# Streaming encoder layer: the convolution's last inputs stored as columns by six DMAs, and memory keys' turns, last sums and first second-layer weight splits put in another order

## The chip, the cores and the metric

The kernel runs on one core of one Trainium2 chip. The metric is the device time of one execution in microseconds (us). The time before is 979.41 us, the median of three runs (978.93 to 979.56). Engines are named as in the profile: PE is TensorE's matmuls and PEld its weight loads, DVE is VectorE, ACT ScalarE, POOL GpSimd, SP SyncE, which here only issues DMAs. A "q" behind an engine's name (SPq, ACTq) marks an instruction of its sequencer, such as a DMA's issue.

## The reference

One layer of an encoder serves two groups at once: a prompt of 512 rows and a sample of 64 rows with caches, both of width 1024, with shared weights, all in float32. What matters here:

- `proj = rmsnorm(x) @ w_in` gives, among others, 1536 channels for a short causal convolution over 4 rows. Beside its result the convolution returns its last three input rows, `conv_new = xp[:, L:]`, a (3, 1536) array for each group. These are two of the outputs.
- The convolved channels feed a gated-delta attention with 4 heads (in chunks of 64 rows). A second attention takes the difference of two softmaxes, normalizes each head's result by its root mean square, and both together go through `w_out` and are added to `x`.
- A cross attention to 256 memory rows follows. For the prompt, its keys and values are projected from the memory: `(m @ wk, m @ wv)`, two (256, 1024) arrays that are also outputs.
- Then `h + relu(hn @ w_ff1)^2 @ w_ff2` with 4096 hidden channels, and a last rmsnorm.

## The kernel before

**Layout.** Activations are kept with channels on the 128 partitions and the 576 rows (512 + 64) along the free dimension. To keep float32's accuracy with the faster float32r matmuls, an operand is split in a high part (a cast on ScalarE) and a low part (the rest, a subtraction on VectorE), and three products are added: high x high, high x low, low x high. `split_weights` (line 155 on) loads a block of weights through SyncE, casts it (line 161) and subtracts (line 162); `project` runs the matmuls of a block of 128 output channels over the rows in two halves (256 and 320) and hands the two results in PSUM to a function that evacuates them. Nearly all matmuls have line 107, the helper `mm`; nearly all turns (transposes on TensorE with an identity) line 113, the helper `tr`.

**PSUM.** The eight banks carry tags: three "pr" for projections, two "ba" for turns and small products, and one each of "g0", "g1" and "gs".

**The order of the work** isn't written out by hand for most of the kernel. The framework takes each instruction's place in the text as its priority and makes one fixed order per engine from it, with its own estimate of when inputs are ready; `tc.high_priority()` lifts a block, `pin` keeps a matmul behind the earlier ones of its engine, and `tc.issue_after(ins)` queues those instructions of a block that run on `ins`'s engine behind `ins`, in order of issue only. At run time each engine, and each DMA queue, takes its instructions in that fixed order and waits at each for its inputs and buffers.

**The convolution's last inputs.** For each of the 12 blocks of 128 channels, GpSimd copies the last three prompt columns and the last three sample columns into `cst`, a [128, 12, 6] tile (lines 461 and 462). After the gate values `gg` and `beta` (up to line 551), the loop at line 553 turns four blocks at a time into a "ba" bank, six rows by 512, copies them to SBUF on VectorE (line 558), and stores three rows to each group's output through SyncE (lines 559 and 560). Around it in time stand the turns of the gate columns (`abT`, line 502 and after, read by TensorE through line 113), the gate chain on VectorE and ScalarE (lines 507 to 551), and the projection of `z` (`project_z`).

**The last attention head and the memory.** `diff_head` works off one head of the second attention, leaves each tile's sum of squares in `so` and its result in `on`, and returns `finish`, which makes the scaling factors (line 1103, then the power on GpSimd, line 208), scales `on` (line 1105), turns it with five turns in two "ba" banks and writes `od` (line 1111). The loop over `w_mem_k` and `w_mem_v` (from line 1137) projects the memory in two column halves `f`. Each half takes four blocks of weights (`kc`), twelve matmuls each. The result is copied to `tokens` (line 1153); a half of the keys is then turned, four turns per "ba" bank and two banks per half, and each bank is split into high and low part (`split_turned`, lines 1131 and 1132); then the half is stored (line 1166). `finish` of the last head comes after the second half of the keys. While the values' first half is done, `od` is split (lines 201 and 202).

**The feed-forward block.** The first layer is done in 16 pairs of output blocks (`ff1_pair`), each with seven products in banks "ba", "gs" and "g1" (a fast scheme with seven products in place of eight). Intermediate results are kept by copies on ScalarE (`keep`, line 1462), and four `put`s do the additions, relu, square and the split of the result (lines 1470 to 1477). The second layer's weights come by `weights2`: a load into one of three `r` buffers (line 1432), a cast (line 1426) and a subtraction (line 1427). From the fourth block on they are split with high priority.

**The end.** The last rmsnorm needs the sums of squares of each row. `final_roots` adds, for the last three row tiles, the sum over `accs[0]` and the sum over the last block's squares (`more`) in one PSUM group, with one matmul each per row tile, then scales (line 1579), takes the power on GpSimd (line 208), and `put_out` scales the turned rows (lines 1563 and 1565) and stores them.

Of the kernel before, what the change touches and what calls it, by code (L numbers as in the profile page):

```python
# [11 lines left out]
ALU = mybir.AluOpType  # L12
# [25 lines left out]
def hybrid_layer_kernel(  # L38
# [61 lines left out]
    def bank(tag="ba"):  # L100
        return ps.tile([P, 512], F32, tag=tag, name=nm(tag), bufs=BANKS[tag])
# [448 lines left out]
    V.reciprocal(beta, t1)  # L550
    halves_of(beta2, beta)

    for j in range(3):
        b = bank()
        for i in range(4):
            tr(b[:6, i * P : (i + 1) * P], cst[:, 4 * j + i, :])
        cso = small("ko", [6, 512])
        V.tensor_copy(cso, b[:6, :])
        nc.sync.dma_start(o_conv_p[0, 0][:, j * 512 : (j + 1) * 512], cso[0:3])
        nc.sync.dma_start(o_conv_s[0, 0][:, j * 512 : (j + 1) * 512], cso[3:6])  # L560

    gsum = bank()
    ggf = gg.rearrange("p c h -> p (c h)")
# [496 lines left out]
    def diff_head(h, between):  # L1060
# [5 lines left out]
        for t in (4, 0, 1, 2, 3):  # L1066
# [32 lines left out]
            A.activation(pr[1][:, :P], po, AF.Square, accum_out=so[:, t : t + 1])  # L1099
            A.copy(on[:, t, :], po)  # L1100

        def finish():
            V.tensor_scalar(so, so, 1.0 / P, EPS, ALU.mult, ALU.add)
            rpow(co, so)
            V.tensor_tensor(on, on, co.unsqueeze(2).to_broadcast([P, 5, P]), ALU.mult)
            b, b2 = bank(), bank()
            for t in range(4):
                tr(b[:, t * P : (t + 1) * P], on[:, t, :])
            tr(b2[:, :P], on[:, 4, :])
            for src, ts_ in ((b, slice(0, SEQ)), (b2[:, DEC:P], slice(SEQ, T))):  # L1110
                A.activation(od[:, h, ts_], src, AF.Identity, scale=dn)
# [22 lines left out]
    mkv = pair(1, F32R)  # L1134
    mkT, mv, tokens = view(mkv, 0, KT, NMEM), view(mkv, 1, 2, D), view(e3, 1, 2, D)
    mkl, mvl = lows("At0", "At1", "Dt0", "Dt1"), lows("Y0", "Y1", "B1", "B1")
    for w, out in ((w_mem_k, o_mk), (w_mem_v, o_mv)):
        dst = tokens
        for f in range(2):
            fs = slice(512 * f, 512 * f + 512)  # L1140
            bs = [bank("pr") for _ in range(2)]
            for kc in range(4):
                wt = split_weights(w[0, 256 * kc : 256 * kc + 256, fs], [P, 2, 512])
                for k in (2 * kc, 2 * kc + 1):
                    for t in range(2):
                        ts_ = slice(t * P, (t + 1) * P)
                        for j, (wi, x) in enumerate(((0, mh), (0, ml), (1, mh))):
                            mm(
                                bs[t], x[:, k, ts_], wt[wi][:, k % 2, :],
                                start=(k == 0 and j == 0), stop=(k == KT - 1 and j == 2),  # L1150
                            )
            for t in range(2):
                (A.copy if t else V.tensor_copy)(dst[:, t, fs], bs[t])
                if out is o_mv:
                    A.copy(mv[:, t, fs], dst[:, t, fs])
                    V.tensor_tensor(mvl[2 * t + f], dst[:, t, fs], mv[:, t, fs].bitcast(F32), ALU.subtract)
            if out is o_mk:
                for i in range(2):
                    b = bank()
                    for j in range(2):  # L1160
                        m = 4 * f + 2 * i + j
                        for t in range(2):
                            tr(b[:, j * 256 + t * P : j * 256 + (t + 1) * P], dst[:, t, m * P : (m + 1) * P])
                    m = 4 * f + 2 * i
                    split_turned(mkT[:, m : m + 2, :], mkl[m // 2].rearrange("p (j n) -> p j n", j=2), b)
            nc.sync.dma_start(out[0, 0].rearrange("(b p) h d -> p b (h d)", p=P)[:, :, fs], dst[:, :, fs])
            if out is o_mk and f == 1:
                finish()
            if out is o_mv and f == 0:
                ob = pair(5, F32R)  # L1170
                for h in range(H):
                    split_to((ob,), od[:, h, :], h, 0)
# [249 lines left out]
    def split(src, tag, bufs, urgent):  # L1422
        shape = list(src.shape)
        wh, wl = (ft(tag + x, shape, bufs, F32R) for x in "hl")
        with tc.high_priority() if urgent else ExitStack():
            A.copy(wh, src)  # L1426
            V.tensor_tensor(wl, src, wh.bitcast(F32), ALU.subtract)  # L1427
        return wh, wl
# [4 lines left out]
        return split(raw, "w2", 3, urgent)  # L1433

    NG, SCALED = 8, 5

    def ff1_pair(p, sx):
        ws = parts.pop(p)
# [53 lines left out]
        put(1, N1, s3, s5)  # L1492
        product(4, x, False)
        put(1, N0, x[:, :NH], None)
        if p + 1 < 2 * NG:
            split_pair(p + 1)
        if p + 2 < 2 * NG:
# [72 lines left out]
    def final_roots(ts, pin=False, more=None):  # L1570
# [2 lines left out]
        r, r2 = tiny([P, 8]), tiny([P, 8])  # L1573
        for i, t in enumerate(ts):
            q0, n = QT[t]
            mm(b[:, t : t + 1], accs[0][:, q0 : q0 + n], ones[:, 0:1], stop=more is None, pin=pin and i == 0)
            if more is not None:
                mm(b[:, t : t + 1], more[:, q0 - 256 : q0 - 256 + n], ones[:, 0:1], start=False)
        V.tensor_scalar(r[:, c], b[:, c], 1.0 / D, EPS, ALU.mult, ALU.add)  # L1579
        rpow(r2[:, c], r[:, c])  # L1580
        return r2

# [97 lines left out]
```

## Time and profile before

| | |
|---|---|
| runs | 978.93, 979.41, 979.56 us |
| profiled execution | 979.89 us |
| its span, from the first to the last instruction | 978.2 us |
| mean granted clock of TensorE | 0.997 |
| last matmul's end | about 8 us before the end of the span |

The profiled execution is one that the hardware profiler recorded; its own time stands 1.7 us above its span. A row of a timeline gives the start in us from the span's start, the duration in us, the engine, the line of the kernel, the operation, output and inputs by tile name, the shapes, the number of instructions merged in the row, and in brackets the idle time of the engine just before, with the instruction whose end ended it. A wait is put down to what came last. Matmuls run pipelined, so their rows overlap; the distance between starts says what one costs.

### The profile page before, as it was taken

How to read it: one execution, taken by the hardware profiler on the slowest of the kernel's cores; microseconds unless marked ns; L12 is line 12 of the kernel's file. 1: busy time of each engine (PE TensorE's matmuls, PEld its weight loads, DVE VectorE, ACT ScalarE, POOL GpSimd, SP SyncE). 2: the span in 40 equal slices, each digit the busy share in tenths (PEclk: the TensorE clock that was granted, in tenths of full speed). 3: DMA queues.
4: the chain of work that ended last, by engine and by line, in shares of the span. 5: the costliest groups of instructions: out<-in, count | busy, mean ns of one | idle time of the engine just before them, and what ended most of it. 6: DMA issues, size and time to landing. Idle time of an engine off the chain costs nothing.

```text
span 978.2 us, 16971 instructions
## 1 busy us (share of the span) xinstructions
PE 960.9 (98%) x6399; PEld 889.0 (91%) x6399; DVE 691.4 (71%) x1540; ACT 537.4 (55%) x1218; POOL 57.5 (6%) x125
## 2 busy tenths in 40 slices
PE   9999999999999999999999999999999999999996
PEld 7999999898888878999999998999999999999996
DVE  6655777867767676666657797567867779978674
ACT  7665785444557675445445567665544445545444
POOL 3441020101000000000000000000000000000000
PEclk9999999999999999999999999999999999999998
DMA  7432432121654656341121423322222223233202
GB/s 216 124 124 76 114 105 66 33 55 40 179 132 132 231 159 197 86 130 44 52 58 44 141 70 93 87 87 86 87 87 86 86 87 87 86 88 86 65 23 97
DMA packets 124915, 96.01 MB, mean 98 GB/s; under 512 B 6204, under 2 KB 112846, under 8 KB 124322
## 3 DMA queue, kind: packets, MB, share of 16 engines
q1 hardware_dynamic: 124466, 94.28, 33.2%
q8 instruction: 50, 0.82, 0.3%
q10 hardware_dynamic: 368, 0.66, 0.2%
q14 instruction: 31, 0.25, 0.1%
HBM read 79.93 MB, written 9.75 MB: 92 GB/s over the span
## 4 chain that ended last, share of the span: by engine, by line
PE 86%; DVE 5%; ACT 3%; issue 2%; DMA 2%; POOL 1%; POOLq 0%; ACTq 0%; DVEq 0%; SPq 0%
PE pr L107 53%; PE g L107 11%; PE ba L107 10%; PE gs L107 6%; PE ba L113 3%; PE g L113 2%; DMA raw<-in_w_ff_dram 1%; DMA r<-in_w_ff_dram 1%; POOL tg L208 1%; DVE wl L162 1%; DMA raw<-in_w_mem_o_dram 1%; ACT wh L161 0%; DVE w L1326 0%; PE gs L113 0%; DVE on L808 0%
## 5 line engine op out<-in xcount | busy, mean ns | idle before, releaser
L107 PE MATMUL pr<-u,wh 128*128 128x320 f32 (+2 forms) x1240 | 326.5, 341 | 1.4 <-DVE zr L195 0.9
L107 PEld LDWEIGHTS pr<-u,wh 128*128 128x128 f32 x1240 | 211.9, 188 | 16.9 <-DVE zr L195 1.1
L107 PE MATMUL pr<-u,wl 128*128 128x256 f32 (+1 forms) x816 | 225.8, 301 | 0.0
L107 PEld LDWEIGHTS pr<-u,wl 128*128 128x128 f32 x816 | 150.0, 189 | 2.2 <-DVE wl L388 0.2
L162 DVE TENSOR_TENSOR wl<-raw,wh 128x1024 fp32r<-128x1024 f32 x65 | 79.5, 1223 | 56.0 <-ACT wh L161 55.8
L161 ACT CAST wh<-raw 128x1024 fp32r<-128x1024 f32 x65 | 68.2, 1050 | 59.9 <-PE pr L107 43.9
L107 PE MATMUL pr<-u,w2h 128*128 128x320 f32 (+1 forms) x384 | 98.5, 340 | 0.0
L1426 ACT CAST w2h<-r 128x512 fp32r<-128x512 f32 x56 | 34.7, 620 | 89.0 <-PE pr L107 85.8
L107 PE MATMUL pr<-f,w2h 128*128 128x320 f32 (+1 forms) x288 | 74.4, 341 | 0.2 <-DVE u L1513 0.2
L107 PEld LDWEIGHTS pr<-u,w2h 128*128 128x128 f32 x384 | 65.0, 188 | 4.5 <-ACT u L1509 0.3
L107 PE MATMUL pr<-u,w2l 128*128 128x256 f32 (+1 forms) x256 | 65.1, 295 | 0.0
L1511 DVE TENSOR_TENSOR u<-u,pr 128x256 f32<-128x256 f32 x96 | 42.4, 450 | 17.0 <-PE pr L107 16.3
L107 PE MATMUL ba<-u,wl 128*128 128x288 f32 x360 | 53.0, 296 | 0.9 <-ACT keep L1462 0.9
L107 PEld LDWEIGHTS pr<-f,w2h 128*128 128x128 f32 x288 | 48.7, 188 | 4.2 <-issue 1.4
L107 PEld LDWEIGHTS ba<-u,wl 128*128 128x128 f32 x360 | 49.2, 188 | 1.7 <-ACT keep L1462 1.6
L107 PE MATMUL pr<-f,w2l 128*128 128x256 f32 (+1 forms) x192 | 48.8, 295 | 0.0
L107 PEld LDWEIGHTS pr<-u,w2l 128*128 128x128 f32 x256 | 46.9, 188 | 1.5
L208 POOL TENSOR_TENSOR tiny<-tiny,nhalf 128x1 f32<-128x1 f32 (+4 forms) x10 | 9.1, 913 | 643.4 <-DVE tiny L1579 531.5
L1427 DVE TENSOR_TENSOR w2l<-r,w2h 128x512 fp32r<-128x512 f32 x56 | 38.5, 688 | 11.2 <-ACT w2h L1426 10.9
L107 PE MATMUL pr<-wh,u 128*128 128x512 f32 x128 | 41.4, 398 | 0.0
L1471 ACT ACTIVATE c<-c 128x288 f32<-128x288 f32 x48 | 20.6, 443 | 29.5 <-DVE c L1470 29.5
L107 PEld LDWEIGHTS pr<-f,w2l 128*128 128x128 f32 x192 | 35.2, 188 | 1.1
(551 smaller groups left out, 2022.2 us busy)
## 6 DMA issues: line engine op xcount, KB each, us to landing
raw<-in_w_ff_dram SPq DMA_DIRECT2D x36, 512.0 KB
raw<-in_w_in_dram SPq DMA_DIRECT2D x28, 512.0 KB
r<-in_w_ff_dram SPq DMA_DIRECT2D x56, 256.0 KB
raw<-in_w_mem_k_dram SPq DMA_DIRECT2D x8, 512.0 KB
raw<-in_w_mem_v_dram SPq DMA_DIRECT2D x8, 512.0 KB
raw<-in_w_out_dram SPq DMA_DIRECT2D x8, 512.0 KB
raw<-in_w_mem_q_dram SPq DMA_DIRECT2D x8, 512.0 KB
raw<-in_w_mem_o_dram SPq DMA_DIRECT2D x8, 512.0 KB
```

The costliest lines, as they stand in the source:

```text
L107: i = nc.tensor.matmul(out, lhsT, rhs, start=start, stop=stop, skip_group_check=skip_group_check)
L113: i = nc.tensor.transpose(out, in_, ident[:n, :n])
L161: A.copy(wh, raw)
L162: V.tensor_tensor(wl, raw, wh.bitcast(F32), ALU.subtract)
L208: G.tensor_tensor(out, in_, bc(nhalf[: in_.shape[0], 0:1], list(in_.shape)), ALU.pow)
L1426: A.copy(wh, src)
L1427: V.tensor_tensor(wl, src, wh.bitcast(F32), ALU.subtract)
L1471: A.activation(c, c, AF.Relu)
L1511: V.tensor_tensor(am, am, b, ALU.add)
```

## The change

Five things are changed.

- The turns of `cst`, their copies and their six stores are gone. Six DMAs on ScalarE's queue write the columns of `cst` directly: for each of the three rows and each group, 128 partitions x 12 numbers, where partition `p` and block `m` go to place `128 m + p` of the output row.
- For the last head, the factors (line 1103 and the power) are traced at the end of `diff_head` instead of in `finish`.
- The turns of the memory keys of a column half are traced in the next half's projection, between its first and second block of weights; the second half's stand in the values' projection, and `finish` of the last head comes behind them. The store of a half no longer stands behind its turns.
- The second-layer splits without high priority (the first three blocks) are queued behind the last instruction of `ff1_pair(1)`'s last `put`, an instruction of VectorE.
- `final_roots` sums `accs[0]` and `more` in two PSUM banks. The first is scaled as before; the second is multiplied and added to it by one VectorE instruction.

```diff
--- before.py
+++ after.py
@@ -550,14 +550,9 @@
     V.reciprocal(beta, t1)
     halves_of(beta2, beta)
 
-    for j in range(3):
-        b = bank()
-        for i in range(4):
-            tr(b[:6, i * P : (i + 1) * P], cst[:, 4 * j + i, :])
-        cso = small("ko", [6, 512])
-        V.tensor_copy(cso, b[:6, :])
-        nc.sync.dma_start(o_conv_p[0, 0][:, j * 512 : (j + 1) * 512], cso[0:3])
-        nc.sync.dma_start(o_conv_s[0, 0][:, j * 512 : (j + 1) * 512], cso[3:6])
+    for i in range(3):
+        for j, dst in enumerate((o_conv_p, o_conv_s)):
+            nc.scalar.dma_start(dst[0, 0, i].rearrange("(m p) -> p m", p=P), cst[:, :, 3 * j + i])
 
     gsum = bank()
     ggf = gg.rearrange("p c h -> p (c h)")
@@ -1099,9 +1094,16 @@
             A.activation(pr[1][:, :P], po, AF.Square, accum_out=so[:, t : t + 1])
             A.copy(on[:, t, :], po)
 
+        def factors():
+            G.tensor_scalar(so, so, 1.0 / P, EPS, ALU.mult, ALU.add)
+            rpow(co, so)
+
+        if h == H - 1:
+            factors()
+
         def finish():
-            V.tensor_scalar(so, so, 1.0 / P, EPS, ALU.mult, ALU.add)
-            rpow(co, so)
+            if h < H - 1:
+                factors()
             V.tensor_tensor(on, on, co.unsqueeze(2).to_broadcast([P, 5, P]), ALU.mult)
             b, b2 = bank(), bank()
             for t in range(4):
@@ -1134,6 +1136,21 @@
     mkv = pair(1, F32R)
     mkT, mv, tokens = view(mkv, 0, KT, NMEM), view(mkv, 1, 2, D), view(e3, 1, 2, D)
     mkl, mvl = lows("At0", "At1", "Dt0", "Dt1"), lows("Y0", "Y1", "B1", "B1")
+    turn_keys = lambda: None
+
+    def key_turns(f, dst):
+        def turn_keys():
+            for i in range(2):
+                b = bank()
+                for j in range(2):
+                    m = 4 * f + 2 * i + j
+                    for t in range(2):
+                        tr(b[:, j * 256 + t * P : j * 256 + (t + 1) * P], dst[:, t, m * P : (m + 1) * P])
+                m = 4 * f + 2 * i
+                split_turned(mkT[:, m : m + 2, :], mkl[m // 2].rearrange("p (j n) -> p j n", j=2), b)
+
+        return turn_keys
+
     for w, out in ((w_mem_k, o_mk), (w_mem_v, o_mv)):
         dst = tokens
         for f in range(2):
@@ -1141,6 +1158,10 @@
             bs = [bank("pr") for _ in range(2)]
             for kc in range(4):
                 wt = split_weights(w[0, 256 * kc : 256 * kc + 256, fs], [P, 2, 512])
+                if kc == 1:
+                    turn_keys()
+                    if out is o_mv and f == 0:
+                        finish()
                 for k in (2 * kc, 2 * kc + 1):
                     for t in range(2):
                         ts_ = slice(t * P, (t + 1) * P)
@@ -1154,18 +1175,8 @@
                 if out is o_mv:
                     A.copy(mv[:, t, fs], dst[:, t, fs])
                     V.tensor_tensor(mvl[2 * t + f], dst[:, t, fs], mv[:, t, fs].bitcast(F32), ALU.subtract)
-            if out is o_mk:
-                for i in range(2):
-                    b = bank()
-                    for j in range(2):
-                        m = 4 * f + 2 * i + j
-                        for t in range(2):
-                            tr(b[:, j * 256 + t * P : j * 256 + (t + 1) * P], dst[:, t, m * P : (m + 1) * P])
-                    m = 4 * f + 2 * i
-                    split_turned(mkT[:, m : m + 2, :], mkl[m // 2].rearrange("p (j n) -> p j n", j=2), b)
             nc.sync.dma_start(out[0, 0].rearrange("(b p) h d -> p b (h d)", p=P)[:, :, fs], dst[:, :, fs])
-            if out is o_mk and f == 1:
-                finish()
+            turn_keys = key_turns(f, dst) if out is o_mk else lambda: None
             if out is o_mv and f == 0:
                 ob = pair(5, F32R)
                 for h in range(H):
@@ -1422,7 +1433,7 @@
     def split(src, tag, bufs, urgent):
         shape = list(src.shape)
         wh, wl = (ft(tag + x, shape, bufs, F32R) for x in "hl")
-        with tc.high_priority() if urgent else ExitStack():
+        with tc.high_priority() if urgent else tc.issue_after(put_last[1]):
             A.copy(wh, src)
             V.tensor_tensor(wl, src, wh.bitcast(F32), ALU.subtract)
         return wh, wl
@@ -1433,6 +1444,7 @@
         return split(raw, "w2", 3, urgent)
 
     NG, SCALED = 8, 5
+    put_last = {}
 
     def ff1_pair(p, sx):
         ws = parts.pop(p)
@@ -1492,6 +1504,7 @@
         put(1, N1, s3, s5)
         product(4, x, False)
         put(1, N0, x[:, :NH], None)
+        put_last[p] = nc.cur_bb.bb.instructions[-1]
         if p + 1 < 2 * NG:
             split_pair(p + 1)
         if p + 2 < 2 * NG:
@@ -1573,10 +1586,14 @@
         r, r2 = tiny([P, 8]), tiny([P, 8])
         for i, t in enumerate(ts):
             q0, n = QT[t]
-            mm(b[:, t : t + 1], accs[0][:, q0 : q0 + n], ones[:, 0:1], stop=more is None, pin=pin and i == 0)
-            if more is not None:
-                mm(b[:, t : t + 1], more[:, q0 - 256 : q0 - 256 + n], ones[:, 0:1], start=False)
+            mm(b[:, t : t + 1], accs[0][:, q0 : q0 + n], ones[:, 0:1], pin=pin and i == 0)
         V.tensor_scalar(r[:, c], b[:, c], 1.0 / D, EPS, ALU.mult, ALU.add)
+        if more is not None:
+            b = bank()
+            for t in ts:
+                q0, n = QT[t]
+                mm(b[:, t : t + 1], more[:, q0 - 256 : q0 - 256 + n], ones[:, 0:1])
+            V.scalar_tensor_tensor(r[:, c], b[:, c], 1.0 / D, r[:, c], ALU.mult, ALU.add)
         rpow(r2[:, c], r[:, c])
         return r2
```

## The prediction

> **What bounds the kernel now.** I read the page's busy shares first, then the waits of TensorE, then the stretches that the change touches. On the page:
>
> ```profile
> span 978.2 us, 16971 instructions
> ...
> PE 960.9 (98%) x6399; PEld 889.0 (91%) x6399; DVE 691.4 (71%) x1540; ACT 537.4 (55%) x1218; POOL 57.5 (6%) x125
> ```
>
> TensorE is busy for 98% of the span; all its idle time, the tail included, is 978.2 - 960.9 = 17.3 us. So a microsecond is won in three ways only: TensorE gets less to do, one of its few waits goes, or the tail after its last matmul gets shorter. Work taken off VectorE (71%) or SyncE is worth nothing by itself. The waits of TensorE that the change can reach:
>
> ```profile
> PE ba L107 <- ACT keep L1462: 1.2, 2, 0.9
> PE ba L113 <- DVE At L1132: 1.1, 1, 1.1
> ```
>
> (Columns: total us, times, longest.) The second is at the turning of the memory keys, the first in the first layer of the feed-forward block. The profiled execution took 979.89 us, 1.7 more than its span; the three timed runs have the median 979.41, 0.5 below it. The terms below are differences inside the span, and I take them off the median.
>
> **The convolution's turns go.** The twelve turns of `cst` in TensorE's timeline, each with the row that follows:
>
> ```profile
> 100.09 0.60 PE L113 MATMUL ba<-ident,cst 128*6 128x128 f32 x4
> 100.53 0.38 PE L113 MATMUL g<-ident,u 128*128 128x128 f32 x2
> ...
> 103.88 1.03 PE L113 MATMUL ba<-ident,cst 128*6 128x128 f32 x8
> 104.67 0.47 PE L107 MATMUL pr<-u,wh 128*128 128x512 f32 x1
> ```
>
> Matmuls overlap, so the price is the distance from start to start: 100.53 - 100.09 = 0.44 for four, 104.67 - 103.88 = 0.79 for eight. TensorE loses **1.23 us** of work. VectorE's three copies of line 558 and SyncE's six issues go too; I count them at nothing, because TensorE doesn't wait for them.
>
> **Six DMAs come to ScalarE's queue.** They can't start before the last `cst` copy (GpSimd's row). What then stands on ScalarE, VectorE and TensorE, and two rows on what an issue costs:
>
> ```profile
> 98.08 0.18 POOL L462 COPY cst<-p 128x3 f32<-128x3 f32 x1
> 99.97 1.05 ACT L161 CAST wh<-raw 128x1024 fp32r<-128x1024 f32 x1 [1.64 <-PE pr L107]
> 101.11 1.20 DVE L162 TENSOR_TENSOR wl<-raw,wh 128x1024 fp32r<-128x1024 f32 x1
> 102.24 0.17 DVE L502 COPY p<-p 16x64 f32<-16x64 f32 x1
> 103.04 0.28 SPq L559 DMA_DIRECT2D out_dram<-p  x1
> 103.14 0.23 PE L113 MATMUL ba<-ident,p 16*128 16x16 f32 x1
> ...
> 971.83 0.92 ACTq L1568 DMA_DIRECT2D out_dram<-u  x2
> ```
>
> The inputs are there at 98.26, and ScalarE is idle for the 1.64 us before 99.97, so I put all six issues there. Queued behind them is the cast at 99.97, behind that on VectorE the low part of the same weights (101.11), behind that in VectorE's order the copy at 102.24, and TensorE's turn at 103.14 needs that copy. With the first four turns of `cst` gone, TensorE comes to it at 103.14 - 0.44 = 102.70; the copy ended at 102.41. So a hold of ScalarE is free for 1.64 + 0.29 = 1.93 us; of each further microsecond TensorE waits all.
>
> What is the hold? ScalarE's own issues took 0.92 for two, with a wait for data between them, so 0.46 each is the upper price; SyncE's store of the same rows took 0.28, the lower. Six hold ScalarE for 1.7 to 2.8 us, and TensorE waits 0 to 0.9. I take **0.5**, the middle. It supposes that the queue takes all six without filling. Whether it does, no row of ScalarE shows. For SyncE's queue the trace shows an issue behind large loads, then the packets from 25.14 to 25.80 us, nearly all of 32 bytes, and those from 98.3 to 107.2, nearly all of 512:
>
> ```profile
> 4.01 0.47 SPq L152 DMA_DIRECT2D raw<-in_w_in_dram  x1
> 4.53 2.49 SPq L129 DMA_DIRECT2D u<-in_x_sample_dram  x1
> ...
> DMA packets 1083, 0.09 MB, mean 134 GB/s; under 512 B 970, under 2 KB 1083, under 8 KB 1083
> ...
> q1 hardware_dynamic: 1083, 0.09, 116.1%
> q1 hardware_dynamic: 2104, 1.07, 45.4%
> ```
>
> An issue of the usual 0.47 us took 2.49 with several loads ahead of it: a full queue holds its issuer. A wide packet costs 45.4% x 16 engines x 8.9 us / 2104 = 30.7 ns. In the other stretch 1.161 x 16 x 0.66 = 12.3 us were spent; less 113 wide ones, the 970 small ones took 9.1 ns each. One new DMA moves 128 x 12 = 1536 single numbers of 4 bytes, 96 on each of 16 engines: 0.87 us at the small price, 2.95 at the wide one. If each issue has to wait for the DMA ahead of it, the hold is 0.46 + 5 x 0.87 = 4.8 us or 0.46 + 5 x 2.95 = 15.2, and TensorE's wait 2.9 or 13.3. So the ends are 0 and 13.3; a hold can't gain anything. I stay at 0.5, by the row of ScalarE's own issues, and carry the rest into the rivals. The weight loads share the engines, but these were taken for 45% of this stretch: six times 0.87 us at the small price fits in.
>
> The Trainium skill, "DMA: Bandwidth & Descriptors", section "Rules for kernel authors", speaks against this edit: a last dimension that isn't contiguous becomes one descriptor per element, and should be rearranged instead; its section "Specifications" adds that a transfer under 512 B is read, modified and written. No row of this trace shows such a narrow write to DRAM, so the trace neither bears this out nor denies it. By about 10.5 ns per packet, from its section "Bandwidth", a new DMA would be an estimated 1.0 us by that page; the rows' 9.1 ns are close to it.
>
> **The memory keys' turns move** behind the first quarter of the next projection, and the last head's `finish` with them. Now:
>
> ```profile
> 361.76 0.65 PE L113 MATMUL ba<-ident,u 128*128 128x128 f32 x4 [1.08 <-DVE At L1132]
> ...
> 359.61 0.83 DVE L1105 TENSOR_TENSOR an<-an,ta 128x640 f32<-128x640 f32 x1 [1.28 <-POOL ta L208]
> 360.36 0.75 DVE L202 TENSOR_TENSOR u<-u,u 128x576 fp32r<-128x576 f32 x1
> 361.02 0.69 DVE L1132 TENSOR_TENSOR At<-ba,u 128x512 fp32r<-128x512 f32 x1
> ```
>
> The last four turns need one of the two "ba" banks. It comes free with the subtraction at 361.02, which on VectorE stands behind `finish`'s scaling (that itself waited 1.28 us for GpSimd's power) and a split of line 202. After the change `finish` is traced behind all key turns, so the subtraction needn't stand behind the scaling, and twelve matmuls of the value projection stand ahead of the second half's turns. I count **1.08 us** gained; the bounds are 0 (another of the six uses of the two banks becomes the late one) and 1.08. `factors` of the last head stays where its two instructions stand now and costs nothing. On SyncE, the keys' stores no longer follow the turns in the text, but both only read the tokens; the value rows that overwrite them come after the turns.
>
> **First second-layer splits.** The new edge reaches VectorE alone, since the instruction that it names is VectorE's; the casts on ScalarE have none.
>
> ```profile
> 590.73 0.62 ACT L1426 CAST w2h<-r 128x512 fp32r<-128x512 f32 x1
> 591.25 0.40 ACT L1462 COPY keep<-ba 128x288 f32<-128x288 f32 x1
> 591.70 1.59 PE L107 MATMUL ba<-u,wl 128*128 128x288 f32 x10 [0.89 <-ACT keep L1462]
> ...
> 591.38 0.69 DVE L1427 TENSOR_TENSOR w2l<-r,w2h 128x512 fp32r<-128x512 f32 x1
> 601.21 0.46 DVE L1477 TENSOR_TENSOR u<-c,u 128x288 fp32r<-128x288 f32 x1 [0.15 <-ACT u L1476]
> ```
>
> TensorE's wait at 591.70 is for the copy at 591.25, and ahead of that stands a cast on ScalarE, not one of the subtractions (591.38) that now go behind 601.21. So I count **0**, between -0.5 (the cast goes away after all, and the copy starts at 590.73) and +0.9: the `r` buffers come free some 10 us later, their loads queue later on SyncE, and another wait like this one arises. The three subtractions, 0.69 each, fit ahead of the next group's projections.
>
> **The tail.** The sums between the last squares and the power:
>
> ```profile
> 968.67 0.38 PE L107 MATMUL ba<-ones,tm 128*128 128x1 f32 x2
> 968.92 0.36 PE L107 MATMUL ba<-ones,accq 128*128 128x1 f32 x2
> ...
> 969.59 0.36 PE L107 MATMUL ba<-ones,tm 128*128 128x1 f32 x2
> ```
>
> Five follow each other from 968.67 to 969.59, 0.23 apart. Of these the three of `tm` remain; the two of `accq` can go ahead. Two steps are **0.45 us**; one VectorE instruction stands for another. Bounds 0 (the order stays) and 0.45.
>
> **Sum:** -1.23 + 0.5 - 1.08 + 0 - 0.45 = -2.26, so 979.41 - 2.26 = 977.15, told as **977.2**.
>
> **The rivals.** *The queue fills, small price* (20%): TensorE waits 2.9, the DMAs cost more than the turns did, in all -2.76 + 2.9 = +0.1: 979.5. For it: 576 packets per engine on one queue, and the 2.49 us above. Against: no row shows ScalarE's queue full. *The queue fills and narrow writes are slow* (19%): at 30.7 ns TensorE waits 13.3, in all +10.5: 989.9, slower. It decides, by over 0.2% (1.96 us), once the wait is over 1.96 + 2.76 = 4.7, a hold of 6.6 us, so from 12.8 ns per packet on. Against: 9.1 ns for the small reads. The skill's rule on narrow writes, named above, would work in this way. *The keys' wait only moves* to another bank (9%): 978.2. *The casts' wait goes too* (7%): 976.7. That the change doesn't do what it says holds for the casts, and is in the forecast.
>
> **Chances.** The forecast has 45%, over 976.3 to 978.0. A difference under 0.2%, about 2 us, can't be told from none here. Faster: most of the forecast (37%), the casts' case (7%), a little of the first rival (3%): 47%. Within 0.2%: the forecast's rest (8%), most of the first rival (14%), the keys' case (8%): 30%. Slower: the slow writes (19%) and what is left of the others (4%): 23%. The range is 975.6 to 982.5: the lower end is all bounds on the good side (-1.23 - 1.08 - 0.5 - 0.45 = -3.3) and 0.5 for waits elsewhere that shrink; above the upper end lies most of the slow writes' case, some 14%, and below the lower one 4%.
>
> **What would show it.** New issues on ScalarE right behind the last `cst` copy, about 0.4 us each: right; issues of a microsecond and more, and TensorE waiting near 103 us: a queue rival. No wait of TensorE for line 1132's subtraction: the keys' term. The wait of 0.89 behind `keep` still there: the casts' term. Three sums between the last squares and the power: the tail. Wrong altogether: new waits of TensorE where nothing was edited, since the order on the engines is made anew for the whole program.

## The result, and the profile after

The changed kernel takes **1004.57 us** (median of four runs, 1001.71 to 1006.06); the kernel before took 979.33 beside it (978.93 to 979.56). The ratio is 1.025, with a 95% interval of 1.0239 to 1.0262: slower by 25 us, where 977.2 had been forecast. In a second set of four runs the same kernel took 1000.27 (999.58 to 1003.21), a ratio of 1.022 [1.0204, 1.0235].

The page of the profiled execution (1005.09 us):

```profile
span 1003.4 us, 16951 instructions
...
PE 967.0 (96%) x6387; PEld 895.7 (89%) x6387; DVE 689.5 (69%) x1534; ACT 534.0 (53%) x1216; POOL 58.4 (6%) x129
...
PEclk9999778999999999999999999999999999999999
...
q10 hardware_dynamic: 9680, 0.69, 4.9%
```

TensorE has 12 matmuls fewer and is busy for longer (967.0 against 960.9), and it stands idle for 1003.4 - 967.0 = 36.4 us where it was 17.3. The clock dips in slices 5 to 7, from about 100 to 175 us. So the loss is in one place; the waits of TensorE name it (total us, times, longest):

```profile
PE ba L107 <- DVE gg L547: 5.4, 1, 5.4
PE ba L113 <- DVE p L502: 5.2, 1, 5.2
PE pr L107 <- DVE u L195: 4.9, 1, 4.9
PE g L107 <- DVE Y L694: 4.7, 1, 4.7
```

All four lie between 104 and 155 us, and none was there before. The engine in such a row is only the last link of a chain. ScalarE's timeline of the same stretch shows the first one:

```profile
98.27 0.45 ACTq L555 DMA_DIRECT2D out_dram<-cst  x1
...
98.88 0.81 ACTq L555 DMA_DIRECT2D out_dram<-cst  x1
...
99.71 7.63 ACTq L555 DMA_DIRECT2D out_dram<-cst  x2
107.44 1.04 ACT L161 CAST wh<-raw 128x1024 fp32r<-128x1024 f32 x1 [7.59 <-issue]
107.46 15.65 ACTq L555 DMA_DIRECT2D out_dram<-cst  x2
123.15 0.63 ACT L459 ACTIVATE u<-p 128x512 f32<-128x512 f32 x1 [14.66 <-issue]
```

The first two issues take 0.45 and 0.81 us; the other four 23.28 together. From 99.71 to 123.1 ScalarE does one cast and otherwise holds an issue. "<-issue" behind the idle time says that the engine waited for its own sequencer. The chain from there to TensorE's first wait, the one of 5.2 us, is the one that the prediction laid out: cast, low part, copy, turn (the timeline of all engines):

```profile
108.52 1.23 DVE L162 TENSOR_TENSOR wl<-raw,wh 128x1024 fp32r<-128x1024 f32 x1 [5.81 <-ACT wh L161]
109.66 0.17 DVE L502 COPY p<-p 16x64 f32<-16x64 f32 x1
...
109.89 0.28 PE L113 MATMUL ba<-ident,p 16*128 16x16 f32 x1 [5.15 <-DVE p L502]
```

The two waits of 4.9 and 5.4 us, which end at 124.7 and 130.8 us, come from the second hold by other links: a copy of line 194 and the activations of the gate chain stand behind it on ScalarE and start only from 123.8 us on.

What the queues moved from 100.3 to 139.8 us, the time of the six DMAs (packets, MB, share of 16 engines; over 100% because the times of packets in flight overlap):

```profile
q10 hardware_dynamic: 9312, 0.04, 118.7%
q1 hardware_dynamic: 2165, 1.09, 37.7%
```

q10 is ScalarE's queue. A narrow write costs 1.187 x 16 x 39.5 / 9312 = **80.6 ns**, measured as the prediction measured its 9.1 and 30.7. This is the mean time of a packet, with those in flight together counted side by side.

The fourth wait is another effect. The decays go to DRAM and come back spread over the partitions; these are SyncE's issues of both, in the changed kernel and in one with the same order and no narrow writes (wide_runs, below):

```profile
132.74 0.31 SPq L571 DMA_DIRECT2D gdram<-p  x1
...
146.73 0.34 SPq L576 DMA_DIRECT2D grow<-gdram  x1
```

```profile
114.83 0.47 SPq L571 DMA_DIRECT2D gdram<-p  x1
118.39 0.34 SPq L576 DMA_DIRECT2D grow<-gdram  x1
```

The second issue waits until the first has landed: 14.0 us in place of 3.6. So a DMA on another queue, of other data, crawls too. And the clock (us; busy time and count of PE, PEld, DVE, ACT and POOL; granted clock, DMA share, GB/s), in the changed kernel and then in wide_runs:

```profile
98.00:160.00 62.00, 40.94 (x210) 37.03 (x209) 24.04 (x83) 24.27 (x43) 4.38 (x6) 0.75 1.24 73
```

```profile
98.00:138.00 40.00, 38.66 (x262) 35.68 (x261) 29.92 (x97) 29.79 (x52) 4.95 (x6) 1.00 0.43 121
```

A matmul of this stage takes 40.94 / 210 = 195 ns in place of 148. Cut finer, the changed kernel shows when (same columns):

```profile
110.00:113.00 3.00, 3.00 (x11) 2.77 (x12) 1.30 (x7) 0.00 (x0) 0.00 (x0) 0.50 2.28 1
...
116.00:120.00 4.00, 3.78 (x23) 3.14 (x21) 0.00 (x0) 0.00 (x0) 0.00 (x0) 1.00 1.75 11
...
134.00:138.00 4.00, 4.00 (x17) 4.00 (x17) 0.32 (x2) 0.00 (x0) 0.00 (x0) 0.50 0.81 25
...
142.00:150.00 8.00, 8.00 (x59) 7.58 (x57) 3.02 (x6) 6.01 (x13) 0.00 (x0) 1.00 0.56 78
```

Right behind a wait of about 5 us TensorE works at half its clock; after some microseconds of unbroken work it is back at 1.00. The Trainium skill, "TensorE: Matmul & The Clock Gate", section "Part 1: The HAM clock gate (the "warmup" mystery)", states this: half rate after an idle window of about 3.4 us, full rate after about as long a busy one. The trace agrees on the half rate. It lasts longer here than the busy window of that page: behind the wait that ends at 109.9 us until about 115, behind the one that ends at 130.8 until about 139. So a wait of this length costs more than its own time. The page of the profile of wide_runs:

```profile
span 974.6 us, 16951 instructions
...
PE 958.1 (98%) x6387; PEld 888.2 (91%) x6387; DVE 689.2 (71%) x1534; ACT 534.6 (55%) x1216; POOL 58.6 (6%) x129
```

The difference between the spans of 28.8 us is 19.9 of idle time, which the four waits account for (20.2), and 8.9 of matmuls at a lower clock; TensorE's matmuls and their order are the same in both.

### The profile page after: what moved, and what is told of

It is laid out like the page before. It is cut to its first block, busy times and chain, and to the rows that moved or that the text cites. A ratio compares the mean times of both kernels' runs of the same rounds, so it can differ in the third digit from the quotient of the medians.

```text
span 1003.4 us, 16951 instructions
## 1 busy us (share of the span) xinstructions
PE 967.0 (96%) x6387; PEld 895.7 (89%) x6387; DVE 689.5 (69%) x1534; ACT 534.0 (53%) x1216; POOL 58.4 (6%) x129
## 4 chain that ended last, share of the span: by engine, by line
PE 57%; issue 2%; DVE 1%; ACT 1%; DMA 0%; POOLq 0%; POOL 0%; ACTq 0%; DVEq 0%; SPq 0%
PE pr L107 36%; PE ba L107 10%; PE g L107 6%; PE gs L107 4%; PE ba L113 1%; DMA raw<-in_w_ff_dram 0%; ACT u L1576 0%; ACT c L1484 0%; DVE u L1532 0%; DVE w2l L1438 0%; ACT c L1483 0%; DVE w L1337 0%; DVE wl L1337 0%; DVE wh L1337 0%; ACT wl L1336 0%
## 5 line engine op out<-in xcount | busy, mean ns | idle before, releaser
L107 PE MATMUL pr<-u,wh 128*128 128x320 f32 (+2 forms) x1240 | 331.7, 346 | 5.0 <-DVE u L195 4.9
L107 PEld LDWEIGHTS pr<-u,wh 128*128 128x128 f32 x1240 | 216.5, 192 | 20.3 <-DVE u L195 5.2
L107 PE MATMUL pr<-u,wl 128*128 128x256 f32 (+1 forms) x816 | 228.6, 304 | 0.0
L107 PEld LDWEIGHTS pr<-u,wl 128*128 128x128 f32 x816 | 153.3, 192 | 2.5 <-DVE wl L388 0.2
```

What stands on the lines that cost most here:

```text
L107: i = nc.tensor.matmul(out, lhsT, rhs, start=start, stop=stop, skip_group_check=skip_group_check)
```

## The experiments

**Which part.** conv_only is the kernel before with the first edit alone; rest_only is the changed kernel with the twelve turns and the row stores of before:

```diff
-    for i in range(3):
-        for j, dst in enumerate((o_conv_p, o_conv_s)):
-            nc.scalar.dma_start(dst[0, 0, i].rearrange("(m p) -> p m", p=P), cst[:, :, 3 * j + i])
+    for j in range(3):
...
```

> The kernel before with the six column DMAs in place of the convolution's turns, and nothing else of the change. Theory 1 (the narrow writes fill ScalarE's queue, and ScalarE is held): all of the loss is here, about 1005 to 1007 us. Theory 2 (one of the other edits brings the loss): about 978.

> The changed kernel with the convolution's turns and their six row stores put back; the other edits stay. Theory 1: between 977 and 979.3, since the last sums give 0.5 us and TensorE's wait at the first second-layer casts is gone. Theory 2: about 1004.

Measured: conv_only 1000.26, ratio 1.0213 [1.0199, 1.0227]; rest_only 977.89, ratio 0.9986 [0.9977, 0.9995]. The whole loss comes with the first edit; the other edits together gain 1.4 us. The first edit also makes the order on the engines anew, in well over a thousand of TensorE's rows, so the next kernels keep the order and change the DMAs alone. conv_only lies 5 us under its expectation, at the value of the changed kernel's second set.

**What about the DMAs.** Four kernels in which the order of instructions on every engine is that of the changed kernel, the DMAs themselves apart, and the changed kernel once more. far_apart, to_sbuf and two_only leave some or all of the two outputs unwritten, and wide_runs writes their numbers to other places:

```diff
 wide_runs: cst laid out [128, 6, 12]
+            nc.scalar.dma_start(dst[0, 0, i].rearrange("(p m) -> p m", p=P), cst[:, 3 * j + i, :])
 far_apart (every8, every32 below: 2 and 8 in place of 16)
+    far = dp.tile([6, 12 * P, 16], F32, tag="far", name="far")
+            nc.scalar.dma_start(far[2 * i + j, :, 0].rearrange("(m p) -> p m", p=P), cst[:, :, 3 * j + i])
 to_sbuf
+    near = const([P, 6, 12, 2], "near")
+            nc.scalar.dma_start(near[:, 2 * i + j, :, 0], cst[:, :, 3 * j + i])
 two_only
-    for i in range(3):
+    for i in range(1):
```

> The changed kernel with the six DMAs in their place, but each writes one run of 48 bytes per partition (128 packets) instead of 12 single numbers (1536 packets): cst is laid out row by row, and the numbers land in another order in the output. The order of instructions on TensorE and VectorE is the same as in the changed kernel. Theory 1: no hold, 976 to 978. Theory 4 (the order): about 1004. Theory 5 (an issue on ScalarE is dear by itself, whatever it moves): about 1000.

> The changed kernel with the six DMAs in their place and of the same count, 1,536 numbers of 4 bytes each, but each number goes 64 bytes from the next, into a scratch tensor in DRAM; the outputs of the convolution's last inputs are not written. Same order of instructions. Theory 1a in its form that neighbouring numbers get into each other's way (16 of them, from several DMA engines, in 64 bytes): fast, 976 to 980. In its form that DRAM takes only so many narrow writes per microsecond: as slow as the changed kernel, 1000 or more.

> The changed kernel with the six DMAs in their place and of the same count of 4-byte packets, but written into SBUF, every second number of a tile; the outputs of the convolution's last inputs are not written. Same order of instructions. If the write to DRAM is what is slow: packets of about 9 ns all along, six DMAs of about 1 us, ScalarE's issues about 0.5 to 1 us, 976 to 978. If narrow packets on a full queue are slow wherever they go: about 1000.

> The changed kernel with only the first two of the six column DMAs, in their place; the other four rows of these outputs are not written. Every engine's order of instructions is that of the changed kernel. Theory 1a (a first stock of about 2,300 narrow writes goes at 9 ns a packet, and only what comes after is slow): 3,072 numbers are little over the stock, ScalarE's two issues take about 0.5 and 0.8 us, 976 to 978. Theory 1b (every narrow write among loads is slow, one alone was fast because of its place): two DMAs of 5 to 6 us each, 979 to 985.

> The changed kernel once more, on the chip of the three others. 1000 to 1006; if the drain of the narrow writes differs from run to run, its time spreads by some microseconds, while the kernel before stays within 1.

Measured: wide_runs 975.82, ratio 0.9964 [0.9952, 0.9977]; far_apart 976.90, 0.9974 [0.9964, 0.9983]; to_sbuf 977.10, 0.9975 [0.9965, 0.9985]; two_only 979.45, 0.9995 [0.9984, 1.0006]; after_again 1000.27, as above. Since wide_runs has the changed kernel's order, the order isn't what costs. The stretch of the six DMAs in far_apart (100.3 to 113.3 us) and in to_sbuf (101.8 to 107.4):

```profile
q10 hardware_dynamic: 9312, 0.04, 64.6%
q1 hardware_dynamic: 1862, 0.94, 41.1%
```

```profile
q10 hardware_dynamic: 9312, 0.04, 88.4%
q1 hardware_dynamic: 177, 0.08, 8.0%
```

The same 9,312 packets cost 14.4 ns each in DRAM when every number lies 64 bytes from the next, and 8.5 ns into SBUF. So neither the count of packets, nor their width, nor the reading of `cst`, nor the issue by itself is the cause. Also, the issues of these two kernels still reach 2.6 and 2.5 us: the queue fills in them as well, and with packets this fast it costs next to nothing.

two_only has no hold, its two issues took 0.45 and 0.81 us as theory 1a had it, and yet its time lies in theory 1b's range, 3.6 us above wide_runs (its runs spread from 976.60 to 981.02). In its trace TensorE waits 2.7 us for the decays, and SyncE's issue of their reading back stands 122.98 - 114.56 = 8.4 us behind that of their writing, where wide_runs has 3.6. So two of these DMAs slow other transfers without holding ScalarE.

**Distance in place.** every8 and every32 put the numbers 8 and 32 bytes apart.

> The changed kernel with the six DMAs of 1,536 single numbers each going into a scratch tensor of DRAM, each number 8 bytes from the next (eight in 64 bytes); the convolution's outputs are not written. Order on the engines as in the changed kernel. Theory A (the chip's memory is slow where several narrow writes fall into the same 64 bytes): as slow as the changed kernel, 995 to 1005, with issues of 2 us and more on ScalarE. Theory B (only writes that touch each other, whole words filled up, are slow): as the kernel with numbers 64 bytes apart, 976 to 978.

> As the one with 8 bytes, but 32 bytes from number to number (two in 64 bytes). Theory A (sharing 64 bytes): between the two, 978 to 990, since two writes share what sixteen share in the changed kernel. Theory B (sharing 32 bytes, or touching): 976 to 978. Theory C (what counts is how small the stretch of memory is that takes the writes): also between the two, and nearer to the kernel with 64 bytes, 977 to 980.

Measured: every8 987.41, ratio 1.0083 [1.0070, 1.0097], a narrow write at 36.7 ns (92.1% of 16 engines for 23.2 us); every32 977.13, ratio 0.9976 [0.9967, 0.9985], 19.7 ns (76.5% for 15.0 us). every8 lies between its two theories and bears out neither. From 32 bytes on the time no longer moves. Sharing 64 bytes is therefore not it: two in 64 bytes are free of the loss. Whether the limit is 32 bytes shared, or how many writes share a place, stays open. So does theory C: the farther apart the numbers lie, the longer is the stretch of memory that takes them, and these kernels write to a scratch tensor instead of the outputs; no run separates this from the distance.

**Distance in time.** In late_apart the six DMAs are issued one by one in the feed-forward stage, 30 to 51 us apart. In spaced they stay in their stage, each behind one of the next six weight casts, 2 to 18 us apart.

```diff
 spaced, in split_weights
             V.tensor_tensor(wl, raw, wh.bitcast(F32), ALU.subtract)
+        if columns:
+            with tc.issue_after(nc.cur_bb.bb.instructions[-2]):
+                nc.scalar.dma_start(*columns.pop(0))
```

> The changed kernel with the same six column DMAs on ScalarE's queue, but issued one at a time in six groups of the feed-forward stage, some 48 us apart, each behind the last ScalarE instruction traced there. The narrow writes are the same, the queue never holds more than one. Theory 1: no hold beyond about 0.5 us per issue, 976 to 978. Theory 3 (the narrow writes take the DMA engines from the weight loads, wherever they are): well over 985. Theory 4 (the fixed order without the turns is a worse one): about 1000.

> The changed kernel with the same six column DMAs of single 4-byte numbers, on ScalarE's queue, in the same stage, but one at a time: each is issued behind one of the next six casts of weights on ScalarE, so 2 to 10 us apart instead of back to back. The order of the other instructions stays that of the changed kernel but for one matmul. Theory A (only a pile-up of these writes is slow): each of the six issues takes 0.4 to 0.5 us, each DMA is through in under 2 us, TensorE's three waits of about 5 us between 105 and 131 us and the one at 155 us are gone, and the time is that of the wide-run and far-apart kernels, 975.5 to 977.5, 2 to 4 us less than before. Theory B (in this stage the writes are slow because the weight loads share the DMA engines, whatever their distance): later DMAs still last 5 us and more, TensorE waits again, and the time is 985 or more. A time between 979 and 984 says that the stores slow the loads of this stage without holding ScalarE.

Measured: late_apart 982.49, ratio 1.0034 [1.0021, 1.0046]; its order differs from the changed kernel's in hundreds of TensorE's rows, so its time can't be charged to the DMAs. spaced 989.03, ratio 1.0099 [1.0085, 1.0113]: theory A's time fell, and theory B's (985 or more) came. The holds did go; all six issues of spaced (min/median/max in ns):

```profile
L165 ACTq DMA_DIRECT2D out_dram<-cst x6: 378/382/447, 98.8 to 147.5; - x6
```

One wait came in their place, on the decays' way through DRAM (SyncE's issues, TensorE's wait and the clock of the ten microseconds around it):

```profile
114.89 0.51 SPq L576 DMA_DIRECT2D gdram<-p  x1
127.66 0.34 SPq L581 DMA_DIRECT2D grow<-gdram  x1
```

```profile
PE g L107 <- DVE Y L699: 8.7, 1, 8.7
```

```profile
130.00:140.00 10.00, 2.12 (x9) 2.13 (x10) 5.00 (x18) 0.38 (x1) 1.78 (x2) 0.70 0.95 171
```

Why so late? Two DMAs of single numbers had been issued by 101 us, and all but three of their packets had been sent by 108.4. From there to 117 the engines moved hardly anything but weight loads (first row; the second is the kernel before, 98 to 102 us):

```profile
q1 hardware_dynamic: 498, 0.25, 71.1%
```

```profile
q1 hardware_dynamic: 1040, 0.52, 48.1%
```

A 512-byte packet took 0.711 x 16 x 8.6 / 498 = 196 ns, against 0.481 x 16 x 4 / 1040 = 30 before. This fits writes that are sent before they are done, and whatever else the DMA engines do creeps until they are.

late_apart shows it for one DMA alone. The packets of the first are sent within 1.1 us of each other, at 7.4 ns each (27.7% of 16 engines for 2.6 us). But the trace has sixteen landing signals for each DMA, and here they come 9.5 to 11.4 us behind the issue; for the first DMA of wide_runs it is 2.2 to 3.0. In between, the packets of SyncE's weight loads take 0.181 x 16 x 7.6 / 374 = 59 ns (622.4 to 630 us), and behind the second DMA 0.403 x 16 x 7 / 286 = 158 (671 to 678). TensorE waits for none of it in that stage. In the changed kernel the last landing signal comes at 146.35 us and the first packet at 100.33: 576 narrow writes per DMA engine took 46.0 us, an estimated 80 ns each, which agrees with the 80.6.

The Trainium skill, "DMA: Bandwidth & Descriptors", section "Back-pressure in remote DMA", says that stalled writes stall the same DMA engine's other queues too; it says it of transfers between cores, and these rows show the like for a core's own writes to DRAM.

**The other edits, one by one**, each alone on the kernel before.

> The kernel before with the memory keys' turns, the last head's factors and its finish placed as in the change, nothing else. Theory A (the wait only moves to another copy of the same keys): a wait of TensorE of about 1.1 us stands near 362 us with another cause than line 1132's subtraction, and the time is that of before within 0.5 us: 978.9 to 979.8. Rival (the prediction's term): the wait goes, 978.3.

> The kernel before with the edge on the first second-layer splits, nothing else. Theory A (the casts get out of the way of the copy into keep after all, because the order on ScalarE is made anew): TensorE's wait of 0.89 us near 592 us is gone, and the time is 0.9 to 1.5 us less: 977.8 to 978.5. Rival (the prediction's term, the edge reaches VectorE alone): the wait stays, 979.3.

> The kernel before with the last sums in the order of the change, nothing else. Theory A (two of the five last steps go ahead): from the first sum of tm to the power on GpSimd it is 1.0 us instead of 1.56, and the time is 0.4 to 0.6 us less: 978.7 to 978.9. Rival: another sum or VectorE's added instruction becomes the last one, 979.3.

Measured: keys_only 979.88, ratio 1.0005 [0.9996, 1.0014]; splits_only 978.38, 0.9988 [0.9979, 0.9997]; sums_only 979.02, 0.9997 [0.9989, 1.0006]. The times are theory A's for the keys (within 0.5 us of the kernel before beside it, 979.62) and for the splits; the sums' 0.6 us lies inside its interval, and their share is read from the profile. The causes are not those that theory A gives. In keys_only the very same subtraction (line 1132, now 1139) is late again:

```profile
360.44 0.83 DVE L1112 TENSOR_TENSOR an<-an,ta 128x640 f32<-128x640 f32 x1 [1.97 <-POOL ta L208]
...
361.18 0.75 DVE L202 TENSOR_TENSOR u<-u,u 128x576 fp32r<-128x576 f32 x1
...
361.85 0.68 DVE L1139 TENSOR_TENSOR At<-ba,u 128x512 fp32r<-128x512 f32 x1
...
362.59 0.44 PE L113 MATMUL ba<-ident,u 128*128 128x128 f32 x2 [1.16 <-DVE At L1139]
```

In splits_only the casts didn't get out of the copy's way: up to the copy, ScalarE has the same instructions in the same order as before. But the first of these casts waits for its load, and that wait is shorter (the kernel before, then splits_only):

```profile
589.39 0.62 ACT L1426 CAST w2h<-r 128x512 fp32r<-128x512 f32 x1 [2.07 <-DMA r<-in_w_ff_dram]
```

```profile
588.47 0.62 ACT L1426 CAST w2h<-r 128x512 fp32r<-128x512 f32 x1 [0.90 <-DMA r<-in_w_ff_dram]
...
590.33 0.40 ACT L1463 COPY keep<-ba 128x288 f32<-128x288 f32 x1
```

What differs is SyncE's queue, again before and then in splits_only:

```profile
582.68 9.78 SPq L1432 DMA_DIRECT2D r<-in_w_ff_dram  x5
```

```profile
584.52 0.92 SPq L1432 DMA_DIRECT2D r<-in_w_ff_dram  x2
598.16 2.07 SPq L1358 DMA_DIRECT2D raw<-in_w_ff_dram  x2
```

Before, three loads into `r` are issued within 2.0 us from 582.68 on. The new edge keeps the first `r` buffer taken (its subtraction runs at 600.73 us in place of 580.56), so the fourth block's load goes behind two weight loads, and the load that the cast waits for has one less beside it. That this is what brings it earlier is an argument; no run separates it. The copy starts 0.92 us earlier than before's 591.25, and TensorE's wait of 0.89 is gone.

**The idea without narrow writes.** one_turn lays `cst` out as [128, 6, 12] and turns it all at once into 72 rows of 128, stored in runs of 512 bytes; one_turn_later has this further down in the text. bounce writes 48-byte runs as wide_runs does, but into scratch memory, and turns them on the way back, with narrow reads in the feed-forward stage:

```diff
 one_turn
+    tr(b[:72, :P], cst.rearrange("p c m -> p (c m)"))
+    cso = small("ko", [72, P])
+    V.tensor_copy(cso, b[:72, :P])
+    for j, dst in enumerate((o_conv_p, o_conv_s)):
+        nc.sync.dma_start(dst[0, 0].rearrange("i (m p) -> (i m) p", p=P), cso[36 * j : 36 * j + 36, :])
 bounce
+        nc.scalar.dma_start(wide[c], cst[:, c, :])
...
+                        nc.sync.dma_start(rows[12 * c : 12 * c + 12, :], wide[c].rearrange("p m -> m p"))
...
+                        nc.sync.dma_start(dst[0, 0].rearrange("i (m p) -> (i m) p", p=P), rows[36 * j : 36 * j + 36, :])
```

> The changed kernel without the column DMAs: the buffer of the last inputs is laid out [128, 6, 12], one turn on TensorE makes 72 rows of 128 of it, one copy takes them out of PSUM, and two DMAs on SyncE's queue write them in runs of 512 bytes. It computes all that the reference does. Theory: twelve turns (1.23 us in the profile of before) become one (about 0.2), no narrow write is left, so about 1 us less than the kernel with the other three edits and the old turns (977.9): 976.3 to 977.5, the fastest of those with all outputs. Rival: the order on the engines is made anew for hundreds of TensorE's instructions behind this place, and new waits eat it up: 978 to 983, as in the kernel with the DMAs late in the feed-forward block.

> As the one with a single turn, but the turn, the copy and the two stores stand in the text behind the decays' last activation instead of ahead of the decays' sums; the order on the engines comes out differently in the stage behind. Same theory, 976.3 to 977.5, and same rival, 978 to 983; if one of the two is fast and the other slow, the order and not the store decides.

> The changed kernel with all its outputs, but by two steps: the six DMAs on ScalarE's queue write the last inputs as they lie, in runs of 48 bytes, into a scratch tensor of DRAM (as in the wide-run kernel); in the feed-forward stage, where SyncE's queue has room, six DMAs read them back turned, as single 4-byte numbers, into 72 rows of SBUF, and two write these in runs of 512 bytes. No 4-byte write to DRAM is left, and the order of all engines but SyncE is that of the changed kernel. Theory (only neighbouring 4-byte writes to DRAM are dear; reading single numbers isn't): the time of the wide-run kernel, 975.2 to 976.6, faster than the kernel before by 0.3 to 0.4% and than the one with the old turns (977.9) by 0.15% and more. Rival (any 9,216 packets of 4 bytes choke the loads beside them): TensorE waits for weights in the feed-forward stage, 980 and more.

Measured: one_turn 987.40, ratio 1.0080 [1.0066, 1.0093]; one_turn_later 985.31, 1.0058 [1.0046, 1.0071]; bounce **975.52**, 0.9961 [0.9947, 0.9974], the fastest of those that write every output, and as fast as wide_runs. The two with one turn were slower even than their rival's 978 to 983. TensorE's order behind the turn is another one, in over a thousand rows; that this and nothing else makes them slow is not shown. In one_turn it is idle for 8.7 of the 152 us from 98 to 250, in rest_only for 2.4 of the 145 up to the same point of the work, which is 6.3 of the 8.4 us between their spans:

```profile
98.00:250.00 152.00, 143.28 (x1058) 130.46 (x1056) 109.81 (x303) 79.47 (x171) 14.08 (x17) 1.00 0.25 67
```

```profile
98.00:243.00 145.00, 142.56 (x1067) 130.89 (x1065) 109.52 (x303) 79.25 (x171) 14.23 (x17) 1.00 0.26 67
```

bounce keeps the changed kernel's order on every engine but SyncE, and its narrow reads do no harm: from 665.9 to 678 us SyncE's queue moved 10,015 packets, 9,304 of them narrow, at 0.605 x 16 x 12.1 / 10015 = 11.7 ns.

```profile
span 973.6 us, 16959 instructions
...
PE 957.5 (98%) x6387; PEld 887.3 (91%) x6387; DVE 688.9 (71%) x1534; ACT 534.2 (55%) x1216; POOL 58.4 (6%) x129
```

## Why the prediction was wrong

**The step that failed** is the hold of ScalarE: "I stay at 0.5, by the row of ScalarE's own issues". It supposed that the queue takes all six DMAs without filling. That row was of the first two issues of ScalarE's queue in the whole run, so it could say nothing of a full one. The runs showed a hold in its place: the third issue is held, ScalarE's six issues take 24.5 us in place of 1.7 to 2.8, and TensorE waits 15.5 us (the first three waits) in place of 0.5. The second rival had the mechanism right, as far as it went: the queue fills, narrow writes are slow, and TensorE waits, first by the chain named. Its price was too small, 30.7 ns as the upper end against 80.6 measured, because both ends came from loads; the trace of before held no row of a narrow write to DRAM. That its wait of 13.3 us lies near the 15.5 is luck. By its own rule, each issue waiting for the DMA ahead, 80.6 ns would give a hold of some 39 us; and of a hold TensorE doesn't wait all, since it had matmuls to do from 110 to 120 us.

The Trainium skill's rules on the page "DMA: Bandwidth & Descriptors", weighed there, pointed the right way. Its section "Rules for kernel authors" has one descriptor per element, and the trace shows one packet per number. That a transfer under 512 B costs a read and a write ("Specifications") would fit the loss, but to_sbuf, far_apart and every32 show that narrow packets alone don't cost it.

**What no rival had**: the crawl of every other transfer (4.7 us of waiting in the changed kernel, 8.7 in spaced), and the lower clock (8.9 us).

**The turns' term** was right as far as the runs can tell. wide_runs, which has neither turns nor holds, is 2.07 us faster than rest_only (1.5 between the profiled spans, 976.1 and 974.6), where -1.23 was forecast for the turns. The rest is about what the intervals leave open, and the two have another order on the engines.

**The keys' term** (-1.08) was wrong: nothing, the size that *The keys' wait only moves* had. That "the subtraction needn't stand behind the scaling" was true of the text and not of VectorE's order, where the scaling stayed ahead of it and came no earlier. VectorE stands idle for 1.97 us ahead of it in keys_only; before, it was 0.43 and 1.28 around the instruction of line 1103. The edit moves that instruction from VectorE to GpSimd, for every head (GpSimd has 129 instructions in place of 125), which neither the list of changes nor the prediction says. In keys_only the wait is still for the same subtraction; in the changed kernel the late one is the evacuation on VectorE behind that subtraction (line 1174, 1.06 us at 386.29).

**The casts' term** (0, bounds -0.5 to +0.9) was wrong too: -1.2 us, between -0.3 and -2.1 by the interval. The edge left the casts' order on ScalarE as it was, as forecast. What it changed is the place of a load: the buffers that come free later, which the prediction counted as a possible loss, are by the reading above what brings an earlier load in sooner, and the wait behind `keep` is gone.

**The tail** was right. In the changed kernel:

```profile
994.44 0.73 PE L107 MATMUL ba<-ones,tm 128*128 128x1 f32 x6
...
995.21 0.16 DVE L1596 SCALAR_TENSOR_TENSOR tiny<-ba,tiny 128x3 f32<-128x3 f32 x1 [1.44 <-PE ba L107]
995.45 0.85 POOL L208 TENSOR_TENSOR tiny<-tiny,nhalf 128x3 f32<-128x3 f32 x1 [15.06 <-DVE tiny L1596]
```

From the first sum of `tm` to the power it is 995.45 - 994.44 = 1.01 us, 1.01 in sums_only too, and 1.56 before: 0.55 less, where 0.45 was forecast. With the DMAs put right, the sum of -2.26 would have been too small a gain: bounce is 3.5 us below before.

## What to carry to other kernels

Price a transfer by a row of the same kind: same direction, same memory, same width and spacing. If there is none, the range has to admit that nothing bounds it, and a small experiment is worth more than the nearest row. Read the price from when the transfer lands, too, and not from its packets alone. Count also what a slow transfer does to its neighbours, since a DMA that nobody waits for can still hold its issuer, every load and the clock. And where one framework makes the order of all engines, compare variants with the same order, or say that the order is part of what was measured.

## What the runs showed of the hardware

- Numbers of 4 bytes written to DRAM side by side, six DMAs in a row, cost 80.6 ns per packet in the changed kernel, 36.7 at 8 bytes' distance, 19.7 at 32, 14.4 at 64; into SBUF 8.5. One such DMA alone sends its packets at 7.4 ns in late_apart, but lands 9.5 to 11.4 us after its issue.
- The price falls due late: in spaced, weight packets took 196 ns in place of 30 for more than 8 us after nearly all narrow packets of the first two DMAs had been sent.
- ScalarE's third issue of 96 packets per DMA engine is the first to be held, in each kernel that sends them back to back (2.6 us in far_apart, 2.5 in to_sbuf); the two ahead of it took 0.4 to 0.9.
- A wait of 5 us costs TensorE some 2 us more afterwards (8.9 us for four), by a clock granted at 0.50 until it has worked for another 5 to 8 us (109.9 to about 115, 130.8 to about 139).
- Why the same kernel took 1004.57 in one set of runs and 1000.27 in another stays open.
